# Entry of the half-size products: first weights through the raw buffers, three input sums by way of DRAM, and the prologue's squares behind the transposes

## The chip, the cores and the metric

The kernel runs on one core of a Trainium2 chip. A time is the duration of one execution on the device in microseconds. The core has a matrix engine (TensorE, PE in the profile; its weight loads are PEld), a vector engine (DVE), a scalar engine (ACT), a general engine (POOL), and a queue of transfers between DRAM and the on-chip memory that SyncE issues (SP, SPq). Each engine carries out its own instructions in order; semaphores make one wait for another.

## The reference

One layer of a generator: tokens x (1024 x 1024) and a context prefix (256 x 1024) are normalised and modulated, one projection gives all streams, and two branches use them: gated linear attention in chunks, in both directions, and differential attention with 16 softmax maps. Gates, two branch projections, a merge, an output projection and the residual follow.

```python
mod_x = jax.nn.silu(c) @ w_ada[layer] + b_ada[layer]
pl = project(modulate(x, sh_x, sc_x), w_in[layer])
pc = project(modulate(ctx, sh_c, sc_c), w_in[layer])
q, k, v, la_f, la_b = gla_streams(pl[0], pl[1], pl[2], pl[4], ...)
s_f = gla_final_state(kc, vc, la_fc)
o_gla = bidir_gla(q, k, v, la_f, la_b, s_f, s_b)
o_diff = diff_attention(q1, q2, [ck1, k1], [ck2, k2], [cv, dv], lam)
out_x = combine(o_gla, pl[3], o_diff, pl[8], pl[9], pl[10], ...)
x = x + g_x * out_x
```

All of it is float32.

## The kernel before

**Products.** An operand v of a product is kept as two rounded parts, hi (a copy by ACT or POOL into the fast type of PE) and lo = v - hi (a subtraction on DVE or POOL). A float32 product is then three matmuls (hi x hi, hi x lo, lo x hi: `mm3`), 128 x 128 by 128 x 512 as a rule. Every weight block of 128 x 512 therefore costs one ACT and one DVE instruction, `w<-raw` and `w<-raw,w` in the profile, between its load and its first product.

**Stages.** Phase A holds the prologue, the projection of the first jobs (keys and queries of the linear attention, C_GK and C_GQ, half of the keys of the other branch, merge gates), the low-rank decays and the preparation of the linear attention (`gla_a`). Then come four groups of "sevens": the value and gate streams (C_GV, C_DV, C_GG, C_DG), each 1024 x 1024 by 1024 x 1024, as seven products of half size. The remaining jobs, the linear attention's second part, the attention and the output follow.

**The prologue.** The ten tiles of tokens (x0 to x7, the two of the context) are squared on ACT (`p<-g`, a sum of squares that goes to POOL, `sm`, for the root), scaled on DVE (`g<-g,sm`), transposed on PE eight blocks of k by three halves (`tp<-ident,g`), modulated on ACT out of the transposes (`p<-tp,shsc`, in `hblock`), and split by POOL (`h<-p`) and DVE (`h<-p,h`). Two `tp` banks alternate, so the transposes of block k + 2 wait for the evacuation of block k. Tiles x0 to x3 belong to half 0. The function `loads` waits for the event `ev_wc` and then runs `xnorm` for tiles 4 to 9, which waits for `ev_md` before its square; `ada(1)` sets `ev_md` when it has evacuated the second half of the modulation.

**The sevens.** The left side of product n is one of a11, a12, s2, s1, s4, s3, a22 (`ORDER`), parts and sums of the quarters of the input; the right side is b11, b21 and so on, quarters of the weight, or sums of them (`BLOCKS`, `weights7`). A product has four steps of k. a11, a12 and a22 are the operands that are there already. `sums7` builds s2, s1, s4 and s3 for each k in four `p` buffers (there are five): four additions hi + lo for four quarters (`p<-h,h`), four additions or subtractions between them (`p<-p,p`), and for each of the results a copy (`s<-p` on ACT) and a subtraction (`s<-p,s` on DVE or POOL). s2 takes the place of a quarter of the input in its tiles (`h<-p`, `h<-p,h`); where the first jobs are not over when it is ready, it waits in DRAM (`d_s2`). The weights of one group go through buffers: `ra` (4 tiles), `rb` (3 tiles) and `rc`, four halves of two of the three raw buffers, which the first jobs use until their last weights are split (`ev_rc` says that they are free). `HELD` says which block goes to `ra` or `rc`; everything else goes to `rb`. b11 is kept until the last product of its group, since b22 - b12 + b11 is formed in its place. `run` in `weights7` splits the blocks in the order of the products into `w` tiles (eight pairs).

**What sets the order.** The program is written by coroutines under a driver (`Driver`) that keeps an estimate of each engine's time, spawns with priorities, and emits an instruction when its turn comes. `yield d.when(x)` resumes near the time at which x is estimated to be ready, `yield On(t, eng)` not before that engine is nearly free. `either` gives an elementwise operation to DVE or POOL, whichever would end first. The order of PE, ACT, DVE and POOL is so fixed when the kernel is built; the framework that builds it places the transfers of SP. All engine operations are recorded by one helper at line 211, matmuls at line 353, transposes at 379, transfers at 318, so the rows of the profile are told apart by their tiles.

Of the kernel before, what the change touches and what calls it, by code (L numbers as in the profile page):

```python
# [9 lines left out]
F32 = mybir.dt.float32  # L10
# [9 lines left out]
P = 128  # L20
# [225 lines left out]
class Hybrid:  # L246
# [183 lines left out]
    def scratch(self):  # L430
# [10 lines left out]
        self.d_aT = [[d(f"d_aT{j}{h}", [2, P, S]) for h in range(4)] for j in range(2)]  # L441
        self.d_bT = [d(f"d_bT{i}", [P, S]) for i in range(8)]
# [92 lines left out]
    def prologue(self):  # L535
# [79 lines left out]
        def ada(part):  # L615
# [31 lines left out]
            if part == 0:  # L647
                d.spawn(ada(1), prio=-1)
            else:
                d.set(ev_md)  # L650
# [51 lines left out]
        for half in (0, 1, 2):  # L702
            idx = [8, 9] if half == 2 else [4 * half + j for j in range(4)]
            for i in idx:
                yield ev_x[i]
            for k in range(NK):
                yield ev_sh[k // 4]
                yield from self.acq("tp")
                pt = self.t("tp", [P, 512])
                for j, i in enumerate(idx):  # L710
                    e = self.tr(pt[:, j * P:(j + 1) * P], xs[i][:, k * P:(k + 1) * P])
                self.d.spawn(hblock(k, half, pt), e)
                yield AtPE(0)
            self.rel("g5", e, len(idx))
# [161 lines left out]
    def phase_a(self):  # L876
# [56 lines left out]
        d.spawn(self.weights7(sevens), prio=3)  # L933
# [19 lines left out]
    HELD = {(0, "b11"): "ra", (2, "b12"): "rc", (4, "b22"): "rc"}  # L953

    def sums7(self):
# [19 lines left out]
        d.spawn(self.raws7(), prio=1)  # L975
        for k in range(4):
            yield from self.acq("p", 4)
            v = {}
            for n, (o, dk, half) in enumerate((("11", 0, 0), ("21", 0, 1), ("22", 4, 1), ("12", 4, 0))):
                v[o] = self.t("p", [P, 512])  # L980
# [20 lines left out]
            for o, y in (("s1", "22"), ("s4", "12"), ("s3", "21")):  # L1001
                yield d.when(v[y])
                hi, lo = self.op7[o, k] = [self.t("s7", [P, 512], F32R) for _ in range(2)]
                self.act.activation(hi, v[y], AF.Copy)
                e = self.either(lo, v[y], hi.bitcast(F32), ALU.subtract)
                d.set(self.ev_op[o, k], e)
            yield ev_s2[k]
            self.rel("p", max(e, ev_s2[k].t), 4)
# [19 lines left out]
    def weights7(self, groups):  # L1028
# [7 lines left out]
        yield self.ev_s  # L1036
# [4 lines left out]
        def load():  # L1041
            for g, (c0, _, _) in enumerate(groups):
# [10 lines left out]
                for n, blocks in enumerate(self.BLOCKS):  # L1053
                    if (g, n) == (0, 1):
                        yield self.ev_rc
# [12 lines left out]
        def sums():  # L1068
            for g, (_, _, ctx) in enumerate(groups):
                for n in range(7):  # L1070
                    for k in range(4):
# [23 lines left out]
                        elif n == 6:  # L1095
# [3 lines left out]
                            self.rel("ra", self.either(b, b, a, ALU.subtract))  # L1099
# [4 lines left out]
        def run():  # L1104
            yield self.ev_w1
            for g, n, k in keys:
# [12 lines left out]
                if n in (3, 5):  # L1119
                    self.rel("rc", e)  # L1120
# [1534 lines left out]
```

## Time and profile before

| | us |
|---|---|
| three runs | 1699.5, 1698.17, 1699.21 |
| median | 1699.21 |
| the profiled execution | 1697.12 |
| its span in the trace | 1695.4 |

| engine | busy us of the span | instructions |
|---|---|---|
| PE | 1635.8 | 8381 |
| DVE | 1203.3 | 1948 |
| ACT | 818.6 | 1633 |
| POOL | 636.3 | 651 |

A row of the timeline gives the start, the time that the group took, engine, line, operation, output <- inputs, the kind, the count, and in brackets how long the engine was idle before and which tile of which engine ended that. A row of the windows gives, for each engine, the busy time and the count in that stretch, then the clock that PE was granted (1.00 is full speed) and the busy share of the transfer engines.

### The profile page before, as it was taken

The numbers are of one execution on the slowest core, as the hardware profiler recorded it, in microseconds if no ns is written. First come the engines' busy times: TensorE is split into PE (matmuls) and PEld (weight loads), VectorE is DVE, ScalarE is ACT, GpSimd is POOL, SyncE is SP. The second block draws the span as 40 slices with busy tenths as digits, with TensorE's granted clock in tenths as the row PEclk, the third lists the DMA queues.
The fourth block names the chain that finished last, engine by engine and source line by source line (L and its number), as shares of the span: only waits on it lengthen the run. The fifth ranks groups of instructions, "written<-read, shape, count | busy, mean of one in ns | idle before, by whom it ended". The sixth has DMA issues, their size and how long they took to land.

```text
span 1695.4 us, 24607 instructions
## 1 busy us (share of the span) xinstructions
PE 1635.8 (96%) x8381; PEld 1354.9 (80%) x8381; DVE 1203.3 (71%) x1948; ACT 818.6 (48%) x1633; POOL 636.3 (38%) x651
## 2 busy tenths in 40 slices
PE   8899999999899999999999989999999999999999
PEld 3687887888688878788888868888888888887887
DVE  4763976875936466757777659888888888847694
ACT  4784555453442344343333336675666666642231
POOL 1600552552300012425543525566665566640000
PEclk9999999999999999999999999999999999999999
DMA  8537545653334475457999674353685534157432
GB/s 306 200 134 233 177 124 187 205 154 130 96 116 151 143 242 160 145 180 233 287 299 299 197 201 113 96 137 104 198 259 139 143 109 132 60 168 267 149 100 75
DMA packets 262975, 290.29 MB, mean 171 GB/s; under 512 B 23193, under 2 KB 185921, under 8 KB 262849
## 3 DMA queue, kind: packets, MB, share of 16 engines
q1 hardware_dynamic: 262848, 288.71, 54.9%
q8 instruction: 66, 1.08, 0.3%
q14 instruction: 61, 0.49, 0.1%
HBM read 192.70 MB, written 95.94 MB: 170 GB/s over the span
## 4 chain that ended last, share of the span: by engine, by line
PE 68%; DVE 14%; ACT 5%; POOL 4%; issue 4%; DMA 3%; SPq 1%; ACTq 0%; DVEq 0%; POOLq 0%
PE mm L353 16%; PE mc L353 9%; PE ma L353 8%; PE s L353 6%; PE mb L353 5%; PE gs L353 5%; PE b L353 4%; DVE sm L211 4%; PE go L353 3%; PE gt L353 3%; PE b L379 3%; PE tp L353 2%; DVE e L211 2%; ACT e L211 2%; POOL sm L211 2%
## 5 line engine op out<-in xcount | busy, mean ns | idle before, releaser
L211 DVE TENSOR_REDUCE sm<-s 128x1 f32<-128x1024 f32 (+1 forms) x192 | 197.4, 1038 | 33.2 <-PE s L353 32.6
L353 PE MATMUL mm<-w,h 128*128 128x512 f32 x864 | 215.4, 398 | 3.1 <-DVE gb L211 2.0
L211 ACT ACTIVATE e<-s,sm 128x1280 f32<-128x1280 f32 x128 | 170.0, 1330 | 85.3 <-DVE sm L211 77.3
L211 POOL TENSOR_TENSOR at<-ac,at 128x512 fp32r<-128x512 f32 x128 | 186.1, 1454 | 10.7
L353 PEld LDWEIGHTS mm<-w,h 128*128 128x128 f32 x864 | 159.5, 188 | 37.6 <-DVE gb L211 2.6
L353 PE MATMUL s<-kk,aq 128*128 128x512 f32 (+1 forms) x768 | 174.0, 360 | 6.9 <-ACT e L211 6.9
L353 PE MATMUL mb<-h,wt 128*128 128x512 f32 x624 | 170.7, 404 | 5.9 <-DVE ft L211 3.2
L211 POOL TENSOR_SCALAR at<-ac 128x512 fp32r<-128x512 f32 x128 | 96.9, 757 | 188.8 <-ACT ac L211 184.7
L353 PE MATMUL mm<-h,w 128*128 128x512 f32 x624 | 156.8, 402 | 3.4 <-DVE w L211 1.8
L353 PEld LDWEIGHTS s<-kk,aq 128*128 128x128 f32 x768 | 121.0, 188 | 26.3 <-ACT e L211 10.6
L353 PEld LDWEIGHTS mm<-h,w 128*128 128x128 f32 x624 | 117.4, 192 | 29.9 <-DVE w L211 3.1
L211 DVE TENSOR_TENSOR w<-raw,w 128x512 fp32r<-128x512 f32 (+1 forms) x117 | 88.2, 782 | 60.9 <-ACT w L211 60.8
L353 PE MATMUL b<-at,vv 128*128 128x256 f32 x960 | 129.8, 283 | 1.7 <-DVE at L211 1.2
L353 PEld LDWEIGHTS mb<-h,wt 128*128 128x128 f32 x624 | 109.6, 189 | 26.7 <-DVE ft L211 4.2
L353 PEld LDWEIGHTS b<-at,vv 128*128 128x128 f32 x960 | 121.1, 188 | 7.1 <-POOL at L211 2.3
L211 POOL TENSOR_TENSOR sm<-sm,nhalf 128x8 f32<-128x8 f32 (+3 forms) x78 | 105.8, 1357 | 30.8 <-DVE sm L211 25.4
L211 DVE SCALAR_TENSOR_TENSOR e<-e,sm,e 128x1280 f32<-128x1280 f32 x64 | 112.3, 1755 | 1.2
L353 PE MATMUL mc<-h,wt 128*128 128x512 f32 x480 | 111.5, 392 | 1.6 <-DVE wt L211 1.6
L353 PEld LDWEIGHTS mc<-h,wt 128*128 128x128 f32 x480 | 89.7, 188 | 21.8 <-DVE wt L211 2.5
L211 ACT ACTIVATE ac<-b 128x512 f32<-128x512 f32 x121 | 71.8, 597 | 57.8 <-PE b L379 55.6
L353 PE MATMUL ma<-w,h 128*128 128x512 f32 x384 | 96.6, 396 | 0.4 <-DVE gp L211 0.4
L379 PE MATMUL b<-ident,e 128*128 128x128 f32 x604 | 87.6, 273 | 6.9 <-DVE at L211 3.1
(380 smaller groups left out, 3151.0 us busy)
## 6 DMA issues: line engine op xcount, KB each, us to landing
raw<-in_w_in SPq DMA_DIRECT2D x37, 512.0 KB, 5.0
rb<-in_w_in SPq DMA_DIRECT2D x64, 256.0 KB, 2.9
aq<-d_qT SPq DMA_DIRECT2D x128, 128.0 KB, 4.0
d_kT<-pl SPq DMA_DIRECT2D x40, 256.0 KB, 2.4
d_dv<-pl SPq DMA_DIRECT2D x40, 256.0 KB, 2.1
kk<-d_kT SPq DMA_DIRECT2D x32, 320.0 KB, 4.7
gv<-d_v SPq DMA_DIRECT2D x40, 256.0 KB, 4.7
vv<-d_dv SPq DMA_DIRECT2D x16, 640.0 KB, 6.7
```

Of the source, the lines that this page charges most:

```text
L211: self.ins = f(out, *args, **kw).ins
L353: self.ins = self.nc.tensor.matmul(out, lhsT, rhs, start=start, stop=stop, skip_group_check=more).ins
L379: self.nc.tensor.transpose(out, src, self.ident[:n, :n])
```

## The change

Three edits, which compute the same values.

1. `ev_md` is set after the last transposes of half 0 (k = 7) in place of `ada(1)`'s evacuation. The squares of x4 to x9 so come after it.
2. b11, the weight of product 0, is loaded into `rc` (the raw halves), and b12 (of products 2 and 3) and b22 (of product 4) into `ra`. `weights7` runs at the start of phase A and no longer waits for `ev_s`; `raws7` is started there too, and `load` waits for `ev_rc` ahead of product 0 and for `ev_s` ahead of product 1. The buffers are released accordingly.
3. `sums7` no longer splits s1, s4 and s3 in place. They are stored to twelve DRAM tensors of 128 x 512 (`d_s7`), loaded one by one into a `p` buffer by `halves` and split by `parts`. The sums of k = 1 and 3 use `pl` buffers in place of `p`, the four quarters' additions are issued when DVE is nearly free, and the buffers are released once the stores are done.

```diff
--- before.py
+++ after.py
@@ -439,6 +439,7 @@
         self.d_qT = [d(f"d_qT{c}", [4, P, 2, S]) for c in range(2)]
         self.d_kT = [[d(f"d_kT{j}{c}", [4, P, T]) for c in range(2)] for j in range(2)]
         self.d_aT = [[d(f"d_aT{j}{h}", [2, P, S]) for h in range(4)] for j in range(2)]
+        self.d_s7 = {(o, k): d(f"d_{o}{k}", [P, 512]) for o in ("s1", "s4", "s3") for k in range(4)}
         self.d_bT = [d(f"d_bT{i}", [P, S]) for i in range(8)]
         self.d_m = [[d(f"d_m{j}{i}", [P, S]) for i in range(8)] for j in range(2)]
         self.d_y = [d(f"d_y{i}", [P, S]) for i in range(8)]
@@ -646,8 +647,6 @@
                 self.rel(tg, e)
             if part == 0:
                 d.spawn(ada(1), prio=-1)
-            else:
-                d.set(ev_md)
             yield from self.acq("gt")
             pt = self.t("gt", [P, 2, 4, m])
             for x in range(2):
@@ -710,6 +709,8 @@
                 for j, i in enumerate(idx):
                     e = self.tr(pt[:, j * P:(j + 1) * P], xs[i][:, k * P:(k + 1) * P])
                 self.d.spawn(hblock(k, half, pt), e)
+                if k == 7 and half == 0:
+                    self.d.set(ev_md)
                 yield AtPE(0)
             self.rel("g5", e, len(idx))
 
@@ -930,7 +931,8 @@
         d.spawn(self.prologue(), prio=-1)
         d.spawn(stream(), prio=9)
         wd2 = self.wstream([(self.win, j[0], j[2]) for j in second], "w", hold=(self.ev_raw, self.ev_w7), end=self.ev_w2)
-        d.spawn(self.weights7(sevens), prio=3)
+        self.weights7(sevens)
+        d.spawn(self.raws7(), prio=1)
         d.spawn(self.prep_lr(), prio=2)
         d.spawn(self.job_lr(), prio=self.PL)
         d.spawn(self.job_la(), prio=1)
@@ -950,7 +952,7 @@
     def seq(ctx):
         return (0, 1, 2, 3, 4, 7, 5, 6) if ctx else range(7)
 
-    HELD = {(0, "b11"): "ra", (2, "b12"): "rc", (4, "b22"): "rc"}
+    HELD = {(0, "b11"): "rc", (2, "b12"): "ra", (4, "b22"): "ra"}
 
     def sums7(self):
 
@@ -972,12 +974,39 @@
                     d.set(self.ev_op[o, k])
         self.d.set(self.ev_s)
 
-        d.spawn(self.raws7(), prio=1)
+        ev_st = [Event() for _ in range(4)]
+
+        def halves():
+            for o in ("s1", "s4", "s3"):
+                for k in range(4):
+                    yield ev_st[k]
+                    yield from self.acq("p")
+                    v = self.t("p", [P, 512])
+                    self.dma(v, self.d_s7[o, k])
+                    d.spawn(parts(o, k, v), d.when(v), prio=2)
+
+        def parts(o, k, v):
+            hi, lo = self.op7[o, k]
+            yield d.on("ACT", v)
+            self.act.activation(hi, v, AF.Copy)
+            yield d.when(hi)
+            e = self.either(lo, v, hi.bitcast(F32), ALU.subtract)
+            d.set(self.ev_op[o, k], e)
+            self.rel("p", e)
+
+        d.spawn(halves(), prio=2)
+        def free(k, tg):
+            yield ev_st[k]
+            yield ev_s2[k]
+            self.rel(tg, max(ev_st[k].t, ev_s2[k].t), 4)
+
         for k in range(4):
-            yield from self.acq("p", 4)
+            tg = ("p", "pl")[k % 2]
+            yield from self.acq(tg, 4)
             v = {}
             for n, (o, dk, half) in enumerate((("11", 0, 0), ("21", 0, 1), ("22", 4, 1), ("12", 4, 0))):
-                v[o] = self.t("p", [P, 512])
+                v[o] = self.t(tg, [P, 512])
+                yield On(0, "DVE")
                 self.either(v[o], x(0, k + dk, half).bitcast(F32), x(1, k + dk, half).bitcast(F32), ALU.add)
             self.store([(self.d_a21[j][k], x(j, k, 1)) for j in range(2)])
             yield d.when(v["21"], v["22"])
@@ -998,14 +1027,11 @@
             else:
                 self.store([(self.d_s2[k], v["11"])], ev=ev_s2[k])
             self.either(v["12"], v["12"], v["11"], ALU.subtract)
-            for o, y in (("s1", "22"), ("s4", "12"), ("s3", "21")):
-                yield d.when(v[y])
-                hi, lo = self.op7[o, k] = [self.t("s7", [P, 512], F32R) for _ in range(2)]
-                self.act.activation(hi, v[y], AF.Copy)
-                e = self.either(lo, v[y], hi.bitcast(F32), ALU.subtract)
-                d.set(self.ev_op[o, k], e)
-            yield ev_s2[k]
-            self.rel("p", max(e, ev_s2[k].t), 4)
+            names = (("s1", "22"), ("s4", "12"), ("s3", "21"))
+            self.store([(self.d_s7[o, k], v[y]) for o, y in names], ev=ev_st[k])
+            for o, _ in names:
+                self.op7[o, k] = [self.t("s7", [P, 512], F32R) for _ in range(2)]
+            d.spawn(free(k, tg), prio=-2)
         yield self.ev_plain
         for k in [k for k in range(4) if late[k]]:
             yield from self.acq("p")
@@ -1033,7 +1059,6 @@
             for n in range(7):
                 keys += [(g, m, k) for k in range(4) for m in ((7, 5) if ctx and n == 5 else (n,))]
         self.w7 = {x: Event() for x in keys}
-        yield self.ev_s
         for x in keys:
             self.w7[x].src, self.w7[x].ready, self.w7[x].done = None, Event(), Event()
         got = {}
@@ -1051,8 +1076,8 @@
                     d.set(ev, e)
 
                 for n, blocks in enumerate(self.BLOCKS):
-                    if (g, n) == (0, 1):
-                        yield self.ev_rc
+                    if g == 0 and n < 2:
+                        yield (self.ev_rc, self.ev_s)[n]
                     for k in range(4):
                         for nm in blocks:
                             yield from get(nm, n, k, self.HELD.get((n, nm), "rb"))
@@ -1096,7 +1121,7 @@
                             b = b[0].x
                             yield self.w7[g, 2, k].done
                             yield d.when(b, a)
-                            self.rel("ra", self.either(b, b, a, ALU.subtract))
+                            self.rel("rc", self.either(b, b, a, ALU.subtract))
                             ready(g, n, k, b)
                         elif n != 3:
                             ready(g, n, k, b[0].x)
@@ -1117,7 +1142,7 @@
                 if n in (1, 6) or n == 5 and groups[g][2]:
                     self.rel("rb", e)
                 if n in (3, 5):
-                    self.rel("rc", e)
+                    self.rel("ra", e)
             d.set(self.ev_w7)
             self.rel("raw", d.now, 2)
             d.set(self.ev_raw)
```

The builder gives an order to each engine. In the prologue, on ACT from the last weight of the modulation on, the kernel before has (`w<-raw` a weight's high part, `p,sm<-g` a square, `p<-tp,shsc` the evacuation of a transposed block):

```order
L211 ACTIVATE w_584<-raw_522 128x512
L211 ACTIVATE w_588<-raw_522 128x512
L211 ACTIVATE p_561,sm_562<-g_115_536 128x1024
L211 ACTIVATE p_563,sm_564<-g_116_538 128x1024
L211 ACTIVATE p_603<-tp_593,shsc_189 128x512
L211 ACTIVATE p_613<-tp_598,shsc_189 128x512
L211 ACTIVATE p_565,sm_566<-g_117_540 128x1024
L211 ACTIVATE p_582,sm_583<-g_118_542 128x1024
L211 ACTIVATE p_647<-tp_629,shsc_189 128x512
L211 ACTIVATE p_653<-tp_634,shsc_189 128x512
```

and the changed kernel has:

```order
L211 ACTIVATE w_588<-raw_534 128x512
L211 ACTIVATE w_592<-raw_534 128x512
L211 ACTIVATE p_606<-tp_596,shsc_201 128x512
L211 ACTIVATE p_609<-tp_601,shsc_201 128x512
L211 ACTIVATE p_629<-tp_623,shsc_201 128x512
L211 ACTIVATE p_639<-tp_634,shsc_201 128x512
L211 ACTIVATE p_649,sm_650<-g_115_548 128x1024
L211 ACTIVATE p_658,sm_659<-g_116_550 128x1024
L211 ACTIVATE p_670,sm_671<-g_117_552 128x1024
L211 ACTIVATE p_672,sm_673<-g_118_554 128x1024
```

The four squares of x4 to x7 moved from among the evacuations of k4 to k7 to behind them.

On ACT at the end of the first job, whose last evacuations are `p<-mm` and `p<-ma` of 128 x 256, and the start of the second job, whose weights are `w<-raw`, the kernel before has (`g` is the decay chain, `gs`, `go`, `gt` its banks):

```order
L211 ACTIVATE g_262_1213<-g_262_1213 128x1280
L211 ACT_TABLE_LOAD
L211 ACTIVATE g_255_1164<-g_255_1164 128x1280
L211 ACTIVATE g_262_1213<-g_262_1213 128x1280
L211 ACTIVATE p_1277<-mm_1242 128x256
L211 ACTIVATE w_1288<-raw_567 128x512
L211 ACTIVATE g_274_1305<-gs_1307,col 128x512
L211 ACTIVATE g_274_1305<-go_1311,col 128x512
L211 ACTIVATE g_274_1305<-gt_1315,col 128x256
L211 ACTIVATE w_1322<-raw_567 128x512
L211 ACTIVATE w_1348<-raw_569 128x512
L211 ACTIVATE w_1358<-raw_569 128x512
```

and the changed kernel has:

```order
L211 ACTIVATE p_1269<-mm_1234 128x256
L211 ACTIVATE w_1281<-raw_573 128x512
L211 ACTIVATE w_1291<-raw_573 128x512
L211 ACTIVATE w_1301<-raw_575 128x512
L211 ACTIVATE w_1312<-raw_575 128x512
L211 ACTIVATE w_1322<-raw_619 128x512
L211 ACTIVATE w_1334<-raw_619 128x512
L211 ACTIVATE g_280_1344<-gs_1346,col 128x512
L211 ACTIVATE g_280_1344<-go_1349,col 128x512
L211 ACTIVATE g_280_1344<-gt_1353,col 128x256
L211 ACTIVATE p_1360<-mm_1267 128x256
L211 ACTIVATE p_1362<-ma_1268 128x256
```

The decay chain's table load and activations of 128 x 1280 stand ahead of the weight splits before; six splits in a row now stand ahead of the next piece of that chain.

At the entry of the sevens, on ACT from the evacuation `p<-ma` ahead of the last products of the first jobs, the kernel before has (`w<-ra` and `w<-rb` weights of products 0 and 1, `s<-p` splits of the sums, `us<-gs` the first evacuation of product 0):

```order
L211 ACTIVATE p_4426<-ma_4354 128x512
L211 ACTIVATE gsc_4438<-gs_4408 128x512
L211 ACTIVATE p_4517<-mm_4424 128x512
L211 ACTIVATE h_169_701<-p_4472 128x512
L211 ACTIVATE s_927_4531<-p_4476 128x512
L211 ACTIVATE w_4535<-ra_4485 128x512
L211 ACTIVATE s_931_4538<-p_4478 128x512
L211 ACTIVATE s_933_4542<-p_4474 128x512
L211 ACTIVATE w_4547<-ra_4487 128x512
L211 ACTIVATE w_4551<-ra_4489 128x512
L211 ACTIVATE w_4555<-ra_4491 128x512
L211 ACTIVATE w_4559<-rb_4493 128x512
```

and the changed kernel has:

```order
L211 ACTIVATE p_4445<-ma_4373 128x512
L211 ACTIVATE w_4457<-raw_4047 128x512
L211 ACTIVATE gsc_4461<-gs_4427 128x512
L211 ACTIVATE w_4471<-raw_4047 128x512
L211 ACTIVATE w_4483<-raw_4048 128x512
L211 ACTIVATE w_4493<-raw_4048 128x512
L211 ACTIVATE p_4540<-mm_4443 128x512
L211 ACTIVATE h_172_742<-p_4513 128x512
L211 ACTIVATE w_4571<-rb_4514 128x512
L211 ACTIVATE us_4544<-gs_4547 128x512
L211 ACTIVATE w_4582<-rb_4516 128x512
L211 ACTIVATE w_4595<-rb_4518 128x512
```

The four weights of product 0 moved ahead of the evacuation `p<-mm`, out of `raw` in place of `ra`, and the three splits of the sums are gone from here. The new transfers stand on SP like this, a little later (`d_s` the new tensors, `d_v` results of product 0 and 1, `rb` and `ra` weights):

```order
L318 DMA d_s_103<-pl_4827 128x512
L318 DMA d_v_76<-p_4847 128x512
L318 DMA ra_4897<-in_w_in 128x512
L318 DMA d_s_111<-pl_4825 128x512
L318 DMA d_v_76<-p_4875 128x512
L318 DMA ra_4904<-in_w_in 128x512
L318 DMA ra_4906<-in_w_in 128x512
L318 DMA d_s_107<-pl_4839 128x512
L318 DMA ra_4911<-in_w_in 128x512
L318 DMA p_4948<-d_s_103 128x512
L318 DMA p_4950<-d_s_104 128x512
L318 DMA p_4952<-d_s_105 128x512
```

Stores of the sums of k = 3 (`pl`) stand among stores of results and loads of weights, and the loads of the sums follow them.

## The prediction

> **What bounds the kernel now.** I read the page first (span, busy shares, instructions), then the windows by stage, then the timelines of the stretches where TensorE (PE) is not full.
>
> ```profile
> span 1695.4 us, 24607 instructions
> ...
> PE 1635.8 (96%) x8381; PEld 1354.9 (80%) x8381; DVE 1203.3 (71%) x1948; ACT 818.6 (48%) x1633; POOL 636.3 (38%) x651
> ```
>
> PE is busy for 1635.8 of 1695.4 us: it is the bound, and a change that leaves its matmuls as they are can win only out of the 60 us in which it waits and out of the matmuls that run at a lower clock. The windows (us from start, length, busy us and count by engine, granted clock, DMA share, GB/s) say where that lies:
>
> ```profile
> 45.00:60.00 15.00, 10.55 (x52) 8.60 (x51) 10.48 (x18) 13.12 (x28) 10.19 (x16) 0.77 0.76 260
> ...
> 123.00:134.00 11.00, 8.05 (x25) 5.04 (x24) 9.61 (x16) 7.27 (x15) 0.00 (x0) 0.84 0.84 287
> ...
> 424.00:434.00 10.00, 5.56 (x13) 4.18 (x14) 9.24 (x14) 6.14 (x12) 3.99 (x2) 0.67 0.32 110
> 434.00:466.00 32.00, 31.14 (x136) 25.11 (x135) 30.17 (x42) 13.04 (x23) 10.02 (x6) 1.00 0.30 92
> ```
>
> Three stretches stand out, with PE idle and its clock down: the prologue, the entry of the second projection job (GLA queries), and the entry of the half-size products. The change touches the first and the last by its text; the second moves because an order built by a simulation shifts.
>
> **Part 1, the squares behind the transposes.** PE and ACT of before, then POOL and DVE:
>
> ```profile
> 45.92 1.10 PE L379 MATMUL tp<-ident,g 128*128 128x128 f32 x8
> 50.53 1.97 PE L379 MATMUL tp<-ident,g 128*128 128x128 f32 x8 [3.51 <-ACT p L211]
> 52.15 0.78 PE L353 MATMUL mm<-h,w 128*128 128x512 f32 x1
> 53.35 2.32 PE L353 MATMUL mm<-h,w 128*128 128x512 f32 x5 [0.42 <-DVE h L211]
> ...
> 59.16 0.86 PE L353 MATMUL mm<-h,w 128*128 128x512 f32 x3
> ```
>
> ```profile
> 46.58 1.15 ACT L211 ACTIVATE w<-raw 128x512 fp32r<-128x512 f32 x2 [1.97 <-DMA raw<-in_w_in]
> 47.64 1.04 ACT L211 ACTIVATE p<-g 128x1024 bf16<-128x1024 f32 x1
> ...
> 49.71 1.43 ACT L211 ACTIVATE p<-tp,shsc 128x512 f32<-128x512 f32 x2
> ```
>
> ```profile
> 51.12 1.63 POOL L211 TENSOR_SCALAR h<-p 128x512 fp32r<-128x512 f32 x2
> ```
>
> ```profile
> 52.21 1.69 DVE L211 TENSOR_TENSOR h<-p,h 128x512 fp32r<-128x512 f32 x2
> ```
>
> Before, two squares (1.04 us each, with their read-outs 2.07 us from 47.64 to 49.71) stand ahead of the evacuations of the transposed blocks k4 and k5, and PE waits 3.51 us for a free bank. After, the evacuation of k4 starts at 47.64 and takes 1.43/2 = 0.72 us; PE transposes k6 at about 48.5 and k7 at about 49.2. The operand of k4 then needs POOL (1.63/2 = 0.82) and DVE (1.69/2 = 0.85): ready at about 48.4 + 0.8 + 0.85 = 50.05, first product at 50.15. From there PE has the 21 products that before lie from 52.15 to 59.16 (first and last rows above) and eight transposes: 21 x 0.23 (11.05 / 48, part 4) + 8 x 0.1 = 5.6 us, so the point reached before at 59.85 (59.16 + 3 x 0.23) is reached at 55.7: **4.1 us gross**. Against it: a stretch at half clock will very likely remain (next paragraph); 3.3 us at half speed costs 1.7. And the squares that now come four in a row behind the evacuations make the scaled tiles of the next half late: four at 1.04 from about 50.6, plus POOL and DVE steps of about 2.5 us, end at 57.2 to 58.5, just when PE has done its products: 0 to 1, taken as 0.5. Net **-2.0** (bounds -3.6, without the slow stretch, and 0: all given back if the squares end 2 us later than I walk them).
>
> The clock first as the trace shows it, at the second job:
>
> ```profile
> 122.50:126.20 3.70, 2.19 (x10) 1.05 (x8) 3.70 (x7) 3.70 (x9) 0.00 (x0) 1.00 0.98 387
> ...
> 126.90:130.20 3.30, 3.30 (x10) 2.59 (x9) 3.06 (x4) 0.01 (x1) 0.00 (x0) 0.52 0.88 228
> ```
>
> PE was busy for 2.19 of 3.70 us there, with no wait over 1.12 us, and still ran the next 3.3 us at 0.52. So gaps of about a microsecond are enough, and I keep the 1.7 us as a loss. The Trainium skill, TensorE: Matmul & The Clock Gate, section on the HAM clock gate, has the half clock come after an idle window of some 3.4 us and go after as much sustained work. By that rule the shortened waits of the prologue would leave the clock alone, and the first part would be worth 3.6 instead of 2.0; the trace speaks against the idle window and for the length of the slow stretch (3.3 us).
>
> **Part 2, the entry of the second job.** Its weights are split by ACT (high part) and DVE (low part) out of raw buffers. Rows of PE and ACT:
>
> ```profile
> 116.90 0.52 PE L353 MATMUL ma<-kk,w 128*128 128x256 f32 x3
> ...
> 122.88 0.63 PE L353 MATMUL mm<-h,w 128*128 128x512 f32 x2
> ...
> 126.20 3.99 PE L353 MATMUL mm<-h,w 128*128 128x512 f32 x10 [1.12 <-DVE w L211]
> ...
> 133.80 2.36 PE L353 MATMUL mm<-h,w 128*128 128x512 f32 x9 [0.24 <-DVE w L211]
> ```
>
> ```profile
> 119.03 2.44 ACT L211 ACTIVATE g<-g 128x1280 f32<-128x1280 f32 x2
> ...
> 121.63 0.62 ACT L211 ACTIVATE w<-raw 128x512 fp32r<-128x512 f32 x1
> ```
>
> The weight buffers come free as the first job passes k (from 116.90 on), but ACT is in the decay chain (activations on g, 119.03 + 2.44 = 121.47), so the first split starts at 121.63 and PE limps. From 122.88 to 133.80 it does 20 products and one decay product set: 20 x 0.23 + 0.6 = 5.2 us of work in 10.9, so 5.7 lost, waits and half clock together. The order of the changed kernel has six weight splits in a row on ACT ahead of that chain, and six low parts on DVE; at 0.52 to 0.6 us each, from 117.6 on, the first is there before PE asks at about 122 and the sixth well ahead. What can remain is the raw reload of the last two k, which waits for splits in front: 0 to 1, taken as 0.2. **-5.5** (bounds -5.9 and 0; it is a re-ordering by the builder's model, and what was moved behind, the decay chain, is due next).
>
> **Part 3, the decay chain's load.** What is due next is the transposition of ge on PE:
>
> ```profile
> 146.96 1.05 SPq L318 DMA_DIRECT2D glab<-d_la  x1
> ```
>
> ```profile
> 164.89 3.94 DVE L211 TENSOR_TENSOR_SCAN glab<-gm,glab 128x645 f32<-128x645 f32 x2
> ...
> 170.95 0.41 DVE L211 TENSOR_TENSOR ge<-gk,ge 128x256 f32<-128x256 f32 x1
> ```
>
> ```profile
> 172.97 0.38 PE L379 MATMUL gt<-ident,ge 128*128 128x128 f32 x2
> ```
>
> PE arrives 7.5 us earlier, at 165.5. The load of the decays stays at about 148 (its store comes behind the same products). Before, the scan waits for nothing of that load but for the weights' split ahead of it on DVE, which moves with PE. Landing at 155 to 156, scans 2 x 2 us and the factors behind them give ge at 161.9 to 163.8: no wait in the middle, 1 us if the load slips by two. Taken **+0.5** (0 to +7.5, the latter giving back all of parts 1 and 2).
>
> **Part 4, the entry of the products.** Rows of PE, then ACT, SP and DVE:
>
> ```profile
> 412.90 11.05 PE L353 MATMUL mm<-h,w 128*128 128x512 f32 x48
> ...
> 428.95 5.06 PE L353 MATMUL gs<-w,h 128*128 128x512 f32 x11 [2.89 <-DVE w L211]
> 433.81 3.10 PE L353 MATMUL go<-w,h 128*128 128x512 f32 x12
> ...
> 454.09 6.02 PE L353 MATMUL mm<-w,h 128*128 128x512 f32 x24 [0.86 <-DVE us L211]
> ...
> 465.38 2.88 PE L353 MATMUL gs<-w,h 128*128 128x512 f32 x12
> ```
>
> ```profile
> 424.88 0.62 ACT L211 ACTIVATE w<-ra 128x512 fp32r<-128x512 f32 x1
> ```
>
> ```profile
> 416.95 1.86 SPq L318 DMA_DIRECT2D ra<-in_w_in  x4
> ```
>
> ```profile
> 416.48 1.88 DVE L211 TENSOR_TENSOR p<-h,h 128x512 f32<-128x512 f32 x3
> ...
> 449.35 1.78 DVE L211 TENSOR_TENSOR w<-ra,w 128x512 fp32r<-128x512 f32 x1
> ...
> 465.76 0.68 DVE L211 TENSOR_TENSOR h<-p,h 128x512 fp32r<-128x512 f32 x1
> ```
>
> Before, product 0's weights are issued at 416.95 and split from 424.88, behind three splits of the sums. PE ends the projection at 423.95 (412.90 + 11.05) and reaches the go block at 433.81; 12 products at 0.23 would have brought it there at 426.7. After, those weights lie in the raw halves long ahead and their splits stand before the last evacuation of the projection on ACT, done at about 420 as w buffers come free from 414 on: **-7.1**. The wait of 0.86 for us at 454.09 and its slow matmuls (6.02 for 24, 5.5 at 0.23) go with DVE's earlier start: -1.2.
>
> Against it stand 24 new transfers (12 stores, 12 loads) and the later split of the sums. They take no engine but SP's queue. A store and a load of 256 KB:
>
> ```profile
> rb<-in_w_in SPq DMA_DIRECT2D x64, 256.0 KB, 2.9
> ...
> d_kT<-pl SPq DMA_DIRECT2D x40, 256.0 KB, 2.4
> ```
>
> One trip is 2.4 + 2.9 us and two splits (0.62 + 0.68), under 7 us, against more than 30 us until the first of these operands (s1) is used, two products behind 433.81. What is late next is the operand s2 of product 2: PE gets there at 465.38 - 8.3 = 457.1 and asks for its last k 2 us later, while before it was ready only at 466.4 (465.76 + 0.68). Before, 61 DVE instructions lie from 416.48 to there (first and last rows above), 50.0 us or 0.82 each with 4 us of idle time among them, 0.75 without. After, some 50 stand between the weight splits that end near 420 and that operand: 457.5 to 461, if all goes as the order has it. I take 1.0 for it and 0.3 for s1: **+1.3** (0 to +5). Part 4 is **-7.0** (-8.3 to -3.3).
>
> **Sum.** -2.0 - 5.5 + 0.5 - 7.0 = -14.0. The profiled execution took 1697.12 us (span 1695.4); less 14.0 is 1683.1. The median shown is 1699.21, 2.1 above the profiled one, so I forecast **1685**. Everything behind product 3 has the same order on PE and I cost it at nothing, since the waits there belong to other chains.
>
> **Rivals.**
> - *Parts 1 and 2 are given back* at the scan chain of part 3, or by the squares: -7.0 alone is left, 1692. For it: the chain's load does not move in the queue. Against: the 10 us between its landing and its use before.
> - *DVE becomes the bound at product 2.* DVE is busy for 30.17 of 32 us from 434 to 466; where POOL works beside it, its row at 449.35 took 1.78 instead of 0.68 us. Four such and 1 us of waits cost 5: -14.0 + 3.7, 1689. The Trainium skill, SBUF: State Buffer, section on who interferes with whom, has a two-input DVE instruction contend with a GpSimd one that reads SBUF; the row agrees.
> - *Slower: the trip through DRAM becomes serial.* SP's queue is in order and the loads share five p buffers with the sums of k 0 and 2. Nine loads stand in a row behind the last sums. If each goes through one buffer (2.9 + 1.3 for the splits + 1.6 for the release and issue = 5.8 us), nine take 52 us from about 463, to 515, when s3 is due by 495: 20 us of PE waits less the 14 won, 1705. It decides once fewer than two buffers are free for the loads; the order of the queue with nine loads following each other speaks against it.
> - *No change.* The weights were early enough and another wait sits at each place: 1699. The releasers in the rows (w, p) speak against it.
>
> **Chances.** Forecast 0.57, given back 0.13, DVE 0.18, serial trip 0.05, no change 0.07. The forecast's own bounds go from 1680.5 (nothing new waits, part 1 at its full 3.6) to 1688; to leave out no more than 2 in 10 the range takes in 1689 and 1692: 1680.5 to 1693. Faster by over 0.2% (3.4 us, about what a measurement of this kernel can tell from no change): 0.57 + 0.13 + 0.18 = 0.88; same 0.07; slower 0.05.
>
> **What would show it.** In the changed kernel's profile: the wait of 3.51 us for p in the prologue is under 1 us, and products start near 50; PE does not wait for w at the start of the second job and the clock there is 1.00; the transposition of ge waits under 1 us; from the end of the projection PE runs into gs without a gap, go follows 2.7 us later; product 2 waits for h under 1 us; no wait for s anywhere. I am wrong if a wait for h or s of several microseconds stands at products 2 to 5, or one for ge near 163.

## The result, and the profile after

| kernel | runs | median us | lowest to highest |
|---|---|---|---|
| before | 4 | 1699.36 | 1698.17 to 1700.3 |
| with the change | 4 | 1687.48 | 1685.7 to 1689.28 |

The ratio is 0.993, with a 95% interval of 0.9913 to 0.9948: 11.9 us less, where the forecast was 1685 in a range from 1680.5 to 1693. The profiled execution took 1685.7 us.

The page of the changed kernel, first lines:

```profile
span 1684.0 us, 24646 instructions
...
PE 1631.7 (97%) x8381; PEld 1354.1 (80%) x8381; DVE 1208.2 (72%) x1940; ACT 819.1 (49%) x1633; POOL 647.8 (38%) x659
```

PE does the same 8381 matmuls in 4.1 us less busy time, with a granted clock of 0.996 over the span instead of 0.993, and the span is 11.4 us shorter. The windows of the changed kernel, the stretches that the prediction showed of before:

```profile
45.00:60.00 15.00, 12.85 (x68) 9.99 (x68) 10.01 (x18) 13.22 (x28) 11.90 (x17) 1.00 0.85 275
...
123.00:134.00 11.00, 11.00 (x50) 9.07 (x50) 7.36 (x8) 8.64 (x12) 0.00 (x0) 1.00 0.54 206
...
424.00:434.00 10.00, 10.00 (x46) 8.29 (x45) 9.24 (x12) 3.12 (x6) 4.70 (x3) 1.00 0.62 219
434.00:466.00 32.00, 29.31 (x127) 23.32 (x126) 25.87 (x32) 14.80 (x27) 12.24 (x8) 1.00 0.67 217
```

PE carries out 68 instead of 52 instructions in the first stretch and 50 instead of 25 in the second, all at a granted clock of 1.00 where before it was 0.77 and 0.84. Only the last stretch has new idle time. Where the 11.4 us arise is seen by setting the same piece of PE's order against itself, start in the one trace and in the other. Rows of PE with the change:

```profile
47.02 1.32 PE L379 MATMUL tp<-ident,g 128*128 128x128 f32 x8 [0.74 <-ACT p L211]
48.10 1.77 PE L353 MATMUL mm<-h,w 128*128 128x512 f32 x6
...
57.29 0.76 PE L379 MATMUL tp<-ident,g 128*128 128x128 f32 x5 [1.14 <-DVE g L211]
57.81 3.50 PE L353 MATMUL gs<-h,pl 128*128 128x512 f32 x14
...
117.33 9.05 PE L353 MATMUL mm<-h,w 128*128 128x512 f32 x39
...
162.12 0.38 PE L379 MATMUL gt<-ident,ge 128*128 128x128 f32 x2
...
262.01 1.10 PE L353 MATMUL gs<-gqr,gkk 128*128 128x64 f32 x8 [3.20 <-POOL gkk L211]
...
404.05 11.05 PE L353 MATMUL mm<-h,w 128*128 128x512 f32 x48
414.93 2.88 PE L353 MATMUL gs<-w,h 128*128 128x512 f32 x12
417.65 2.88 PE L353 MATMUL go<-w,h 128*128 128x512 f32 x12
...
447.57 2.20 PE L353 MATMUL gs<-w,h 128*128 128x512 f32 x9
451.84 0.73 PE L353 MATMUL gs<-w,h 128*128 128x512 f32 x2 [2.07 <-ACT h L211]
...
605.03 2.68 PE L353 MATMUL mm<-w,h 128*128 128x512 f32 x10
610.03 10.55 PE L353 MATMUL mm<-w,h 128*128 128x512 f32 x38 [2.33 <-DVE w L211]
620.42 2.88 PE L353 MATMUL gs<-w,h 128*128 128x512 f32 x12
```

And rows of PE before, at the places that the prediction did not show:

```profile
271.85 1.10 PE L353 MATMUL gs<-gqr,gkk 128*128 128x64 f32 x8 [2.16 <-POOL gkk L211]
...
619.49 11.27 PE L353 MATMUL mm<-w,h 128*128 128x512 f32 x48
630.59 2.88 PE L353 MATMUL gs<-w,h 128*128 128x512 f32 x12
```

| piece of PE's order | before | after | ahead by | gained there |
|---|---|---|---|---|
| transposition of ge | 172.97 | 162.12 | 10.85 | 10.85 |
| last products ahead of the sevens | 412.90 | 404.05 | 8.85 | -2.0 |
| go of product 0 | 433.81 | 417.65 | 16.16 | +7.31 |
| gs of product 2 | 465.38 | 447.57 | 17.81 | +1.65 |
| first block behind the second group | 630.59 | 620.42 | 10.17 | -7.64 |
| end of the span | 1695.4 | 1684.0 | 11.4 | +1.23 |

So the gains were larger than forecast, 19.8 us for 15.8, and 9.6 us were given back at three places: 2.0 around the wait for gkk, 3.5 at products 2 and 3 (2.07 us of waiting for h in the row above, 0.41 us behind it, 0.21 us for s, and the rest in the short groups of products between these waits), and 4.1 from there to the end of the second group, all of it at the group's last product. Only the middle one had been priced.

That last one starts from an order. Rows of DVE, then of ACT, of the changed kernel, and the ACT rows of before at the same place; the split of the product's last weight is `w<-rb`, the evacuations of the product in front are `rope` and `gb`:

```profile
602.47 0.69 DVE L211 TENSOR_TENSOR rope<-rope,mm 128x512 f32<-128x512 f32 x1 [0.24 <-PE mm L353]
603.08 0.68 DVE L211 TENSOR_TENSOR gb<-gb,mm 128x512 f32<-128x512 f32 x1
603.67 0.68 DVE L211 TENSOR_TENSOR rb<-rb,raw 128x512 f32<-128x512 f32 x1
...
606.66 1.64 DVE L211 TENSOR_TENSOR pl<-rope,pl 128x512 fp32r<-128x512 f32 x1 [0.15 <-ACT pl L211]
608.23 1.75 DVE L211 TENSOR_TENSOR w<-rb,w 128x512 fp32r<-128x512 f32 x1
```

```profile
606.00 0.63 ACT L211 ACTIVATE pl<-rope 128x512 fp32r<-128x512 f32 x1 [4.49 <-DVE rope L211]
606.54 0.62 ACT L211 ACTIVATE w<-rb 128x512 fp32r<-128x512 f32 x1
```

```profile
616.58 0.62 ACT L211 ACTIVATE w<-rb 128x512 fp32r<-128x512 f32 x1
...
619.31 0.62 ACT L211 ACTIVATE pl<-rope 128x512 fp32r<-128x512 f32 x1
```

In the changed kernel the weight's sum and its split stand on DVE and ACT behind evacuations that wait for PE, so PE waits for a weight that waits for PE's own earlier block; ACT was idle for 4.49 us in front of it. Before, the split stood 2.9 us ahead of its product (616.58 to 619.49).

The order is not all of it. The last two DVE rows, which end at 609.98 and so end the wait, take 1.64 and 1.75 us where the rows ahead of them take 0.68, while POOL works on a sum of weights for the next group:

```profile
606.45 2.98 POOL L211 TENSOR_TENSOR ra<-ra,raw 128x512 f32<-128x512 f32 x2 [7.14 <-DMA ra<-in_w_in]
```

At 0.68 us each they would be done 2.0 us earlier, so by this estimate most of the 2.33 us comes from POOL beside DVE. The same pair of stretched rows stands ahead of the wait in the kernel with edits 2 and 3 alone; no run takes this POOL work away.

### The profile page after: what moved, and what is told of

Read it like the earlier page. It is cut to its first block, busy times and chain, and to the rows that moved or that the text cites. A ratio compares the mean times of both kernels' runs of the same rounds, so it can differ in the third digit from the quotient of the medians.

```text
span 1684.0 us, 24646 instructions
## 1 busy us (share of the span) xinstructions
PE 1631.7 (97%) x8381; PEld 1354.1 (80%) x8381; DVE 1208.2 (72%) x1940; ACT 819.1 (49%) x1633; POOL 647.8 (38%) x659
## 4 chain that ended last, share of the span: by engine, by line
PE 71%; DVE 11%; POOL 5%; issue 4%; ACT 3%; DMA 2%; SPq 0%; ACTq 0%; POOLq 0%; DVEq 0%
PE mm L353 16%; PE mc L353 10%; PE ma L353 9%; PE s L353 6%; PE mb L353 6%; PE b L353 5%; PE gs L353 5%; DVE sm L211 4%; PE go L353 3%; PE b L379 3%; PE gt L353 3%; DVE e L211 2%; PE tp L353 2%; ACT e L211 2%; POOL p L211 2%
## 5 line engine op out<-in xcount | busy, mean ns | idle before, releaser
L379 PEld LDWEIGHTS b<-ident,e 128*128 128x128 f32 x604 | 72.5, 141 | 23.8 <-ACT ac L211 3.9
```

Of the source, the lines that this page charges most:

```text
L379: self.nc.tensor.transpose(out, src, self.ident[:n, :n])
```

## The experiments

### One edit or two at a time

Each of the three edits moves instructions in a stretch of its own, so parts of the change can be run. The first two kernels are the change without its second and third edit, and without its first. Edit 1 alone:

```diff
-            else:
-                d.set(ev_md)
...
+                if k == 7 and half == 0:
+                    self.d.set(ev_md)
```

> Edit 1 alone (the squares behind the transposes), weights and sums as before. The order of ACT and DVE differs from before only from the prologue to the start of the second job. Theory A: this edit alone makes both the prologue's gain and that of the second job's entry, 10.9 us up to the first transposition of ge, of which 2 are lost at the wait for gkk near 262 us: 8.8 less than before, 1690.6 (1689 to 1692); the first wait of the sevens stays as before (PE idle for about 4.5 us for w, clock down). Theory B: the second job's entry gains through the early start of the weights' tasks, edit 1 only moves the prologue: 4 less, 1695.3. Theory C: what is won early is given back at the sevens' entry, whose loads do not come earlier: 1698 or more.

Measured: 1692.35 us against 1699.01, ratio 0.9953 (0.9938 to 0.9968), 6.7 less. PE reaches the transposition of ge at 163.37, 9.6 earlier than before, with no wait in the second job, and the entry of the sevens is as before:

```profile
163.37 0.38 PE L379 MATMUL gt<-ident,ge 128*128 128x128 f32 x2
...
423.06 4.96 PE L353 MATMUL gs<-w,h 128*128 128x512 f32 x11 [2.89 <-DVE w L211]
```

Theory B and C fall: the edit to the squares alone moves the second job. The median is 1.8 above what theory A had and just outside its range (1688.76 to 1694.09 over four runs).

Edits 2 and 3 without edit 1:

> Edits 2 and 3 without edit 1. Theory A: the entry of the sevens gains 9.0 (7.3 at the first products, 1.7 behind them), product 2 gives back 3.5 (wait for h and half clock), the last product of the second group gives back 4.1 (wait for w) and 1.7 come back two products later: 3 less than before, 1696.4 (1695 to 1698). Theory B: those two waits come only because PE is early through edit 1; alone, the two edits keep all of the 9: 1690.5 to 1692.

Measured: 1695.59 us, ratio 0.9981 (0.997 to 0.9992), 3.4 less: theory A. The wait for h at product 2 and the wait for w at the last product of the second group are there although PE is not early through edit 1:

```profile
461.77 0.73 PE L353 MATMUL gs<-w,h 128*128 128x512 f32 x2 [2.08 <-ACT h L211]
...
621.47 8.91 PE L353 MATMUL mm<-w,h 128*128 128x512 f32 x38 [2.25 <-DVE w L211]
```

So they belong to edits 2 and 3. Together 6.7 and 3.4 make 10.1, against 11.9 for the whole; the difference is of the size of the scatter of these runs.

Edits 1 and 2, and in place of edit 3 the splits of s1, s4 and s3 in place, as before:

```diff
-            self.store([(self.d_s7[o, k], v[y]) for o, y in names], ev=ev_st[k])
...
+                self.act.activation(hi, v[y], AF.Copy)
+                e = self.either(lo, v[y], hi.bitcast(F32), ALU.subtract)
```

> Edits 1 and 2, the sums s1, s4, s3 split in place as before (no trip through DRAM). Theory A: the trip buys time on DVE; with three more splits for each k ahead of the operand s2 of product 2, the wait for h there grows from 2.5 to 6 to 9 us, so 1692.5 (1690 to 1695). Theory B: the 24 transfers and the in-order queue cost more than the splits; without them the time is that of the change or lower: 1687.5 or less.

Measured: 1695.74 us, ratio 0.998 (0.9971 to 0.9989): 8.3 slower than the change, in theory A's direction and beyond its price. PE's rows say where:

```profile
442.31 8.32 PE L353 MATMUL mm<-w,h 128*128 128x512 f32 x24 [3.98 <-DVE us L211]
...
461.51 2.10 PE L353 MATMUL gs<-w,h 128*128 128x512 f32 x3 [3.40 <-ACT h L211]
```

The splits in place delay not only s2 but also the evacuation `us` of product 1, which stands behind them on DVE. What edit 3 buys is room on DVE. The run takes all of edit 3 back, the `pl` buffers and the line that holds the additions with it, so how much of the room is the trip's alone is not shown.

Edit 3 alone:

> Edit 3 alone: sums by way of DRAM, weights of product 0 loaded late through their own buffers as before, squares as before. Theory A: the entry's wait is set by the late load and split of the weights; without the three splits of sums among them it shrinks by some 2 us (three ACT splits at 0.52, three DVE ones at 0.6), product 2's wait stays small: 1696 to 1698. Theory B: the splits of the sums were what held the weights back; the whole 7 us go: 1691 to 1693.

Measured: 1698.0 us, ratio 0.9997 (0.9985 to 1.0009): no difference. PE's waits at the entry are smaller (0.57, 0.23, 0.84 and 0.73 us in place of 1.61 and 2.89), and a new one appears for an operand that made the trip:

```profile
479.66 0.50 PE L353 MATMUL gs<-w,s 128*128 128x512 f32 x1 [2.75 <-DVE s L211]
```

Theory A, with its gain given back at product 3. Edit 3 is worth nothing without edit 2, and edit 2 without edit 3 makes the kernel slower: added to edit 1 it gave 1695.74 us for 1692.35. The rows fit this reading: the early weights take DVE's time from the sums, and the room that edit 3 makes is of use only if the weights are there.

### Is the trip through DRAM hidden?

```diff
                     self.dma(v, self.d_s7[o, k])
+                    self.dma(v, self.d_s7[o, k])
```

> The whole change, but each of the twelve sums is loaded twice from DRAM into the same buffer, one load after the other, so that a trip is longer by a load (2.9 us) and 12 transfers more stand in the queue. Theory A: the trip is hidden, with more than 10 us to spare until s4 and s3 are used: 1687.5 within 1.5, and no wait for s over 0.5 us beyond the 0.2 there is. Theory B: the trips go one by one through few buffers and are close to the bound: 5 us or more of waits for s at products 3 to 5, 1692 or more.

Measured: 1689.67 us (1688.53 to 1690.07), 2.2 above the change; between the two theories. One wait grows, that for the last part of s1 at product 3, from 0.21 to 2.08 us:

```profile
468.75 0.50 PE L353 MATMUL gs<-w,s 128*128 128x512 f32 x1 [2.08 <-DVE s L211]
```

For s4 and s3 nothing changes, so their trips have room for a second load. That of the last s1 has none: it is already on PE's path. This trace also has a slow stretch behind the waits of 2.00 and 0.42 us at product 2 (12 products of go in 4.24 us instead of 2.89), which the changed kernel's trace does not have behind 2.07 and 0.41 us; so PE came to product 3 later, and the wait of 2.08 us is less than the whole delay of s1.

### The wait at the last product of the second group

Only the first group keeps b11 in the raw halves; later groups use the buffers as before:

```diff
-                            yield from get(nm, n, k, self.HELD.get((n, nm), "rb"))
+                            tg = self.HELD.get((n, nm), "rb")
+                            yield from get(nm, n, k, {"ra": "rc", "rc": "ra"}.get(tg, tg) if g else tg)
```

> The whole change, but b11 goes through the raw halves in the first group of sevens only; from the second group on the buffers are as before, and so is the order of ACT and DVE there. Theory A: the wait of 2.3 us for w and the half clock behind it (4.1 us) at the last product of the second group come from the exchanged buffers in later groups (the split of its last weight stands behind an evacuation that waits for PE): they go, and the 1.7 us won two products later may go too: 1683.4 to 1685.1. Theory B: the wait comes because PE is early there, whatever the buffers: 1687.5.

Measured: 1686.86 us (1685.42 to 1687.35), which the runs cannot tell from the change. The wait for w is gone, as theory A says, and with it theory B. But the wait that the kernel before has two products later is back with the old order. Its row, then that of before:

```profile
690.06 10.06 PE L353 MATMUL mm<-w,h 128*128 128x512 f32 x36 [1.95 <-DVE gb L211]
```

```profile
701.02 8.50 PE L353 MATMUL mm<-w,h 128*128 128x512 f32 x36 [1.95 <-DVE gb L211]
```

So the exchange of buffers in later groups causes the wait for w, and trades one wait for another of nearly the same length. In this trace a slow stretch follows the wait for gb (10.06 us for 36 products), in that of before none does (8.50).

### What makes s2 late at product 2

All sums of `sums7` on DVE, none on POOL (six calls of `either`, for the additions, the combinations and the low part of s2; the first is shown):

```diff
-                self.either(v[o], x(0, k + dk, half).bitcast(F32), x(1, k + dk, half).bitcast(F32), ALU.add)
+                self.dve.tensor_tensor(v[o], x(0, k + dk, half).bitcast(F32), x(1, k + dk, half).bitcast(F32), ALU.add)
```

> The whole change, but the sums of the operands (four additions, four combinations for each k) all go to DVE, none to POOL. Theory A: POOL's part costs more than it saves, since a DVE instruction beside a POOL one takes 1.75 to 1.78 us instead of 0.68 (the changed kernel's DVE rows at 416.6, 426.0, 427.7, 439.2, 440.9, 449.4): without it the last step of s2 is ready some 3 us earlier, the waits for h of 2.07 and 0.41 us at product 2 and the half clock behind them go, 1684 to 1685.5. Theory B: DVE is the bound between 416 and 453 us by count; with five more instructions ahead of that step it comes 3 us later and the waits grow: 1689 to 1691.

Measured: 1681.79 us (1681.01 to 1684.48), ratio to before 0.9896 (0.9875 to 0.9917): 5.7 less than the change, more than theory A asked. Product 2 runs without a wait (PE's row), and the windows of the stretch, first of the change, then of this kernel, show why:

```profile
447.64 2.88 PE L353 MATMUL gs<-w,h 128*128 128x512 f32 x12
```

```profile
405.00:453.00 48.00, 45.52 (x201) 37.07 (x199) 43.69 (x56) 18.22 (x32) 17.64 (x13) 1.00 0.65 216
```

```profile
405.00:453.00 48.00, 48.00 (x212) 39.44 (x211) 42.86 (x64) 18.85 (x33) 9.30 (x6) 1.00 0.69 225
```

DVE (fifth and sixth figure: busy time and count) carries out 64 instructions in 42.86 us with POOL at 6, and 56 in 43.69 us with POOL at 13. With seven instructions fewer beside it on POOL, DVE got through eight more in less time. The rows of the changed kernel, DVE and then POOL, show the single case: two DVE instructions of 0.68 us take 1.77 and 1.78 while POOL adds.

```profile
426.00 1.77 DVE L211 TENSOR_TENSOR w<-rb,w 128x512 fp32r<-128x512 f32 x1
427.70 1.78 DVE L211 TENSOR_TENSOR ra<-ra,raw 128x512 f32<-128x512 f32 x1
```

```profile
425.50 3.43 POOL L211 TENSOR_TENSOR p<-h,h 128x512 f32<-128x512 f32 x2
```

The Trainium skill, SBUF — State Buffer, section Who interferes with whom, says that a DVE instruction with two inputs in SBUF contends with a GpSimd one that reads SBUF; both rows are of that kind.

The sums do not account for all of it. The two profiled executions are 4.0 us apart: 2.0 at products 2 and 3 (3.0 won there, 1.0 given back to a wait of 1.21 us for s), and 1.6 at the last product of the second group, where this trace happens to have no slow stretch behind the same wait (last section). The half clock that the expectation puts behind the waits at product 2 is not in the changed kernel's trace either: from 447 to 466 us its granted clock is 1.00.

The second cure is to drop the line that holds the additions back:

```diff
                 v[o] = self.t(tg, [P, 512])
-                yield On(0, "DVE")
                 self.either(...)
```

> The whole change without the line that holds the four additions of each k until DVE is nearly free. The last step of s2 then stands five instructions earlier on DVE, the weights of products 1 to 3 later. Theory A: the wait at product 2 is set by DVE's order alone: it shrinks by 3 us or goes, 1684.5 to 1686. Theory B: the weights take over: a wait for w of 1 to 4 us at product 1 or 2, 1687 to 1690.

Measured: 1682.8 us (1682.43 to 1686.92), ratio to before 0.9898 (0.9875 to 0.9922), theory A and 1.7 us beyond its range. There is no wait for h, with 12 POOL instructions left between 405 and 453 us; the wait for us at product 1 is 1.32 us. So what made s2 late was the additions' place in DVE's order together with POOL's work beside it: taking away either one ends the wait.

Both cures together:

> The whole change with the sums on DVE and without the line that holds the additions back. Theory A: both cures end the same wait (product 2 for h), so they do not add; what the second can still win is the wait for s of 1.2 us at product 3: 1680.5 to 1682. Theory B: the early sums push the weights of products 1 and 2 back, and a wait for w or us of 1 us or more appears: 1683 to 1685.

Measured: 1689.47 us (1688.41 to 1692.36), worse than either, in theory B's direction and far beyond its price. PE's row and DVE's:

```profile
442.06 8.01 PE L353 MATMUL mm<-w,h 128*128 128x512 f32 x24 [4.83 <-DVE us L211]
```

```profile
438.92 2.49 DVE L211 TENSOR_TENSOR pl<-h,h 128x512 f32<-128x512 f32 x4
441.32 0.68 DVE L211 TENSOR_TENSOR us<-us,mm 128x512 f32<-128x512 f32 x1
```

The additions of the last k (2.49 us) now stand ahead of the evacuation `us` on DVE, and PE waits 4.83 us for it and then runs 24 products in 8.01 us instead of 5.5. The last run has the sums on DVE and, from the second group on, the buffers as before (the expectation calls the kernel with the sums on DVE dv7):

> The first-group-only version and the sums on DVE together. Theory A: both effects add: as dv7, with the wait of 2.3 us for w at the last product of the second group gone too: 1683 to 1685. Theory B: neither is on the path that sets the end, and each leaves the time within the scatter: 1686.5 to 1687.5.

Measured: 1683.41 us (1682.31 to 1684.6), ratio to before 0.9903 (0.9883 to 0.9923). That is inside theory A's range, but no better than the sums on DVE alone, as the trade of waits above would have it. The sums on DVE alone have the lowest median of all, 5.7 us below the change and 17.7 below the kernel before, which took 1699.51 us beside it; the runs cannot tell them from the additions at once (1682.8) or from this last kernel.

## Why the prediction was right, and where its terms were off

**Bound.** PE was the bound, and the three stretches named are where it gained, but for some 1.4 us ahead of the second job, most of them at the decay products of the first. Of the signs that the prediction named, the prologue, the second job, ge and the step from gs to go came out; product 2 waited for h 2.07 and 0.41 us instead of under 1, and there was a wait of 0.21 us for s.

**Part 1 (-2.0).** The mechanism held, with the products starting at 48.10 instead of the 50.15 that I walked. At 57.81 PE has 24 transposes and 30 products behind it, 9 more than before at 59.85; less 9 x 0.23 that is 55.7 against 59.85, 4.1 earlier (0.7 of it was there already at 45.92, where this execution is at 45.19), so 3.4 in place of 2.0. The waits for the scaled tiles, some 1.4 us in place of 0.5, are in it already, and the earlier start of 2.0 paid for them. The term that failed is the cost that I took off for a slow stretch, 1.7: here it did not arise, and the window from 45 to 60 has a clock of 1.00. The rule of the Trainium skill that I had set against the row (TensorE: Matmul & The Clock Gate, Part 1: The HAM clock gate) has the half clock come after an idle window of some 3.4 us; with waits of 0.74 to 1.14 us this trace agrees with it. It is luck all the same: of the nine kernels with edit 1, three have the slow stretch there, after waits of 1.15 to 1.35 us, far below that window, and a fourth waited 1.25 us without it. The window of the one that loads the sums twice:

```profile
45.00:60.00 15.00, 13.28 (x65) 10.91 (x66) 9.64 (x17) 13.33 (x28) 11.24 (x15) 0.89 0.87 279
```

Nor would it have cost 1.7. From the transposes (45.19 here) to the same point (57.81) those three take 13.1 to 13.2 us and the other six 12.4 to 13.1, because PE then waits 0.2 to 0.6 us for the scaled tiles instead of 1.4: the two costs overlap, and I had added them.

**Part 2 (-5.5).** Right in place and mechanism: no wait at the second job, clock 1.00, and edit 1 alone does it. PE was 5.55 us ahead at its first product (117.33 for 122.88) and 10.85 at the transposition of ge, so the part gave 5.3. Between the prologue's 4.1 and these 5.55 lie some 1.4 us that no part had forecast.

**Part 3 (+0.5).** No wait for ge appeared at 162.12. The step that failed is that I looked for the chain's answer only at its load: PE was late 100 us further on, at the products that take gkk, where the wait grew from 2.16 to 3.20 us and the slow stretch behind it, which before has too, was longer: the 12 products `mm<-h,w` there took 5.30 us for 4.20. Up to the last products ahead of the sevens that made 2.0. The same place costs 2.98 us of waiting in the kernel with edit 1 alone. What would bring gkk earlier was not tried.

**Part 4 (-7.0).** The entry gave 7.31 for a forecast of 7.1, and 1.65 for 1.2. The term for late operands was mis-sized: 1.3 forecast, 3.5 measured, inside the bound of 5 and with the rival's mechanism, POOL's sums stretching DVE's, in part. Taking them away ends the wait, and so does issuing the additions earlier with POOL still at work. The room for the trip through DRAM, which I had put at more than 30 us for s1, is nothing for its last part; the doubled load shows it. That part is stored only with the last sums, and its load is the first of the nine behind them:

```profile
453.56 0.33 SPq L318 DMA_DIRECT2D d_s<-pl  x1
...
454.42 14.95 SPq L318 DMA_DIRECT2D p<-d_s  x9
```

**Behind product 3 (0).** This was the step that failed outright: I called the waits there other chains' own. The exchange of buffers goes on in every group, and it moved the orders of ACT and DVE at the end of the second one: 4.1 lost, 1.2 won back by the end. The run that keeps the exchange to the first group shows that it is the exchange; how much of the wait is POOL's work beside DVE is only estimated.

That the sum came close is in part luck, since two errors cancelled: the gains were 19.8 for 15.8, the losses 9.6 for 1.8 (0.5 in part 3 and 1.3 in part 4). As for the rivals: DVE at product 2 was there at a lower price than the 5 us I gave it; the gains of parts 1 and 2 were given back by 2.0 of 10.9; the serial trip did not happen, as the nine loads were issued within 14.95 us, where 5.8 each would have been 52.

## What to carry to other kernels

Where the order of in-order queues is computed at build time, an edit's effect has to be looked for at every place at which its buffers turn over, not only at the one that it was made for: compare the two orders around each evacuation that waits for the engine that is the bound. A second engine that helps with elementwise work is worth it only if the first does not slow down beside it; count what the first carries out in the stretch with and without. And two cures for one wait need not add: here the additions, early and all on DVE, stood ahead of another instruction that PE also needs, and PE waited 4.83 us for it.

## What the runs showed of the hardware

A DVE subtraction of 128 x 512 with both inputs on chip takes 0.68 us alone and 1.77 to 1.78 beside a POOL addition (rows from 425.50 to 427.70 above), so each POOL addition of 1.7 us cost the DVE instruction beside it 1.1 us.

Whether a short wait brings the half clock was not a matter of its length alone. After 2.33 us of waiting the changed kernel's PE took 10.55 us for 38 products. At the same place, with the sums on DVE, a wait of 2.21 us was followed by the same products in 8.91 us; with both cures a shorter wait, 2.12 us, was followed by 10.52:

```profile
607.52 8.91 PE L353 MATMUL mm<-w,h 128*128 128x512 f32 x38 [2.21 <-DVE w L211]
```

```profile
614.08 10.52 PE L353 MATMUL mm<-w,h 128*128 128x512 f32 x38 [2.12 <-DVE w L211]
```

What decides between the two is not shown, nor how often either comes in executions of one kernel, since each kernel has one trace. A forecast of a single wait like this one can be off by 1.6 us for that reason alone.
